# Hybrid encoder trunk on one core: activation operands start 16 to 240 bytes past multiples of 256, and the activation sums are issued over five steps per pair

## The chip, the cores and the metric

One NeuronCore of one Trainium2 chip runs the whole program. The metric is the device time of one execution in microseconds; the median of the kernel before is 2223.44 us (three runs, 2222.92 to 2223.47).

## The reference, cut to what matters

The input is 256 tokens of width 2048 in float32. Layer 0 is a mixer of a bidirectional mLSTM and an RG-LRU, layer 1 is dilated attention, and each is followed by a SwiGLU feed-forward block of width 5632. Nearly all the work is products of activations with weights that are read once from HBM.

```python
for l in range(DEPTH):                       # DEPTH = 2
    h = rmsnorm(x, e_norm[e])                # l = 0
    x = x + even_mixer(h, e_w_in[e], ..., e_w_out[e])
    ...
    h = rmsnorm(x, o_norm[o])                # l = 1
    x = x + dilated_attention(h, o_w_qkv[o], o_w_o[o])
    ...
    h = rmsnorm(x, f_norm[l])
    x = x + swiglu(h, f_w1[l], f_w3[l], f_w2[l])
return rmsnorm(x, final_norm)

def swiglu(h, w1, w3, w2):
    return (jax.nn.silu(h @ w1) * (h @ w3)) @ w2
```

## The kernel before

**Numbers.** Each float32 operand is split into two float32r parts, a high part (ScalarE copies, which rounds) and a low part (VectorE subtracts the high part). A product is then three matmuls on TensorE: high by high, high by low, low by high. Activations are split once when they are made; weights are split as they arrive from HBM, 1 MB (four blocks of 128 rows by 512 columns) at a time.

**Steps.** The program is a list of 768 steps, each half of such a weight block. `emit_step(s)` first issues the splits of the weights for steps up to s + 3 (`AHEAD = 3`, four buffers each for the high and the low parts, so that the split for step s + 4 needs the buffer that step s reads), then the matmuls of step s, then calls `run_tasks` once. There are three kinds of step:
- narrow (536 steps of 12 matmuls): a 128x128 block of activations is the stationary operand, 512 columns of weights move;
- wide (112 steps of 16 matmuls): weights are stationary, and the activations move, 512 and then 256 columns;
- seven (120 steps of 21 matmuls): in the first product of each feed-forward block (all columns but the first chunk's, blocks 4 to 15 of the width), a 2x2 block product is done with seven products of 256 columns in place of eight. It needs sums of weights (`weight_sums`, made together with the split of that block) and sums of activations (`act_sums`).

**Tasks.** Everything that isn't a weight split or a main matmul is a Python generator. `run_tasks` moves each generator on to its next `yield`: first those in `urgent` (evacuations of finished chunks), then up to three of `queue`. What a generator issues between two yields thus stands behind the matmuls of one step and ahead of the splits that the next step issues. Each engine works through its own instructions in the order issued. `until(flag)` calls `run_tasks` again and again until a flag is set, at the moment when the matmuls that need it are issued.

**The sums of activations.** `act_sums` is put in the queue at the first step of each feed-forward block (step 112 for the first). For each of six pairs of width blocks (4, 6, 8, 10, 12, 14) it adds the high and low parts (L1067, VectorE), forms four sums (L1070 to L1073, VectorE), and splits them (L1074 ScalarE, L1075 VectorE): one pair per `run_tasks`. The first chunk of the feed-forward block has 16 narrow steps (112 to 127). The second begins with four more narrow ones; its seven steps are 132, 133, 136, 137, 140 and 141, and they need the pairs in order, pair 1 at step 132 and pair 6 at step 141. In the last step of a chunk (141), the order of the seven products is another: the first one is `sa(0)`, which reads a sum.

**Addresses.** In SBUF, all the tiles that hold activations as operands of these matmuls (`xT`, and the slots of `hT`, `ya`, `yb`, `oT` and `sf`) begin at multiples of 256 bytes, and so do the weight tiles. A slot is 2112 floats (8448 bytes) and the tiles named take 2048 of them. The mLSTM's values `v` stand in a slot with heads 258 floats apart, so all but the first head of a row block begin off a multiple of 256.

Of the kernel before, what the change touches and what calls it, by code (L numbers as in the profile page):

```python
# [9 lines left out]
F32 = mybir.dt.float32  # L10
# [6 lines left out]
S = 256  # L17
P = 128
# [22 lines left out]
SPLIT_BUFS = 4  # L41
AHEAD = 3

SLOTS = 8
SLOT = 2112
EV_BUFS = 10
# [22 lines left out]
def trunk_kernel(ctx: ExitStack, tc: tile.TileContext, a, out):  # L69
# [14 lines left out]
    mxp = ctx.enter_context(tc.tile_pool(name="mxp", bufs=2, space=PSUM))  # L84
    ctx.enter_context(tc.manual_schedule())

    def slot(shape, dt=F32, name="s8"):
        t = s8p.tile([P, SLOT], dt, tag="s8", name=name)
        n = int(np.prod(shape))
        v = t[:, :n]  # L90
        if len(shape) == 1:
            return v
        pat = {2: "p (a b) -> p a b", 3: "p (a b c) -> p a b c", 4: "p (a b c d) -> p a b c d"}[len(shape)]
        return v.rearrange(pat, **dict(zip("abcd"[1:], shape[1:])))
# [44 lines left out]
    ehr = const.tile([MH, MH, P], F32R, name="ehr")  # L139
    ident, upper, lower = cst[:, 0, :], cst[:, 1, :], cst[:, 2, :]  # L140
    ones = const.tile([P, P], F32, name="ones")
    xT = const.tile([P, KB, 2, S], F32R, name="xT")
    hgh = const.tile([P, 16], F32, name="hgh")[:, :RB]

    def transpose(o, i, n=P):
# [408 lines left out]
    def gr_block(b):  # L554
        def gen(ch):
            if b % 4 == 0:
                rg["g"] = m4((4, S), "gr")
            t = rg["g"]
            g = t[:, b % 4, :]
            join(ch.acc[0], g)  # L560
            ch.acc = None
            V.tensor_tensor(g, g, cur["rB"], op=ALU.mult)
            yield
            if b % 4 < 3:
                return
            yield
            A.activation(t, t, AF.Gelu_apprx_tanh)
            yield
            b0 = b - 3
            while not {f"rgh{b0 // 2}", f"rgh{b0 // 2 + 1}"} <= flags:  # L570
                yield
            yt = ys["y", 8 + b0] = slot((4, 2, S), F32R, name="yb")
            V.tensor_tensor(t, t, rg["h"][:, b0:b0 + 4, :], op=ALU.mult)
            yield
            A.copy(yt[:, :, 0, :], t)
            yield
            V.tensor_tensor(yt[:, :, 1, :], t, yt[:, :, 0, :].bitcast(F32), op=ALU.subtract)
            for k in range(4):
                flags.add(f"y{8 + b0 + k}")
            yield  # L580

        return gen
# [233 lines left out]
    def ml_out(c):  # L816
        while not {f"mh{2 * c}", f"mh{2 * c + 1}", f"go{c}"} <= flags:
            yield
        rs = sm(4, "mrs").rearrange("p (a b) -> p a b", a=2)
        V.tensor_scalar(rs, ml["ss"][:, :, 2 * c:2 * c + 2], 1.0 / DV, EPS, op0=ALU.mult, op1=ALU.add)  # L820
        rsf = rs.rearrange("p a b -> p (a b)")
        power(rsf, rsf, 4)
        yield
        yt = slot((4, 2, S), F32R, name="ya")
        ys["y", 4 * c] = yt
        es = []
        for t in range(2):
            y = ev("ya")
            for k in range(2):
                h = 2 * c + k  # L830
                V.scalar_tensor_tensor(
                    y[:, k * DV:(k + 1) * DV], ml["h"][:, t, h, :], rs[:, t, k:k + 1],
                    ml["go"][:, t, h * DV:(h + 1) * DV], op0=ALU.mult, op1=ALU.mult,
                )
            es.append(y)
        yield
        yield from lag()
        for p in range(2):
            ps = tp("yT")
            for k in range(2):  # L840
                for t in range(2):
                    f0 = (2 * p + k) * P
                    transpose(ps[:, k, t * P:(t + 1) * P], es[t][:, f0:f0 + P])
            for k in range(2):
                kb = 2 * p + k
                g = hgh[:, 4 * c + kb:4 * c + kb + 1]
                A.mul(yt[:, kb, 0, :], ps[:, k, :], g)
                V.scalar_tensor_tensor(
                    yt[:, kb, 1, :], ps[:, k, :], g, yt[:, kb, 0, :].bitcast(F32), op0=ALU.mult, op1=ALU.subtract
                )  # L850
                flags.add(f"y{4 * c + 2 * p + k}")
            yield
# [80 lines left out]
    def att_head(h):  # L933
        qk, v, ab = at.pop(("qk", h)), at["v", h // 4], at.pop(("bias", h))
        if h % 4 == 0:
            at["o", h // 4] = slot((4, 2, S), F32R, name="oT")
        yield
        yield from lag()
        yield from take()
        ps = mx("asc")  # L940
        for t in range(2):
            tk = slice(t * P, (t + 1) * P)
            mm3(ps[:, t * S:(t + 1) * S], (qk[:, 0, tk], qk[:, 1, tk]), (qk[:, 2, :], qk[:, 3, :]), True, True)
        yield
        sn = ev("asn")
        st = sm(6, "ast")
        for t in range(2):
            V.tensor_tensor_reduce(
                sn[:, t * S:(t + 1) * S], ps[:, t * S:(t + 1) * S], ab[:, P - t * P:P - t * P + S],
                1.0, 3e38, op0=ALU.add, op1=ALU.min, accum_out=st[:, t:t + 1],  # L950
            )
            A.activation(
                sn[:, t * S:(t + 1) * S], sn[:, t * S:(t + 1) * S], AF.Exp, scale=-1.0, bias=st[:, t:t + 1],
                accum_out=st[:, 2 + t:3 + t],
            )
        give()
        V.reciprocal(st[:, 4:6], st[:, 2:4])
        for t in range(2):
            V.tensor_scalar(
                sn[:, t * S:(t + 1) * S], sn[:, t * S:(t + 1) * S], st[:, 4 + t:5 + t], None, op0=ALU.mult  # L960
            )
        yield
        yield from lag()
        pt = tp("apT")
        for k in range(2):
            for t in range(2):
                transpose(pt[:, k, t * P:(t + 1) * P], sn[:, t * S + k * P:t * S + (k + 1) * P])
        pv = m4((2, CW), "apv", F32R)
        split2(pv, pt.rearrange("p a b -> p (a b)"))
        yield  # L970
        yield from lag()
        yield from take()
        po = mx("apo")
        hs = slice(h % 4 * DH, h % 4 * DH + DH)
        for k in range(2):
            ks = slice(k * S, (k + 1) * S)
            mm3(po[:, :S], (v[:, 0, k, hs], v[:, 1, k, hs]), (pv[:, 0, ks], pv[:, 1, ks]), k == 0, k == 1)
        yield
        split2(at["o", h // 4][:, h % 4], po[:, :S])
        give()  # L980
        flags.add(f"ao{h}")
        yield
# [6 lines left out]
    def ffn(l, gains, nxt):  # L989
# [29 lines left out]
        def up3(c):  # L1019


            def gen(ch):
                while f"up{l}_{c}" not in flags:
                    yield
                es = st.pop(("e", c))
                for t in range(2):
                    V.scalar_tensor_tensor(
                        es[t], ch.acc[t], cur["rstd"][:, t:t + 1], es[t], op0=ALU.mult, op1=ALU.mult
                    )
                ch.acc = None  # L1030
                yield
                yield from lag()
                h = st["h", c] = slot((4, 2, S), F32R, name="hT")
                for p in range(2):
                    ps = tp("hTp")
                    for k in range(2):
                        f0 = (2 * p + k) * P
                        for t in range(2):
                            transpose(ps[:, k, t * P:(t + 1) * P], es[t][:, f0:f0 + P])
                    A.copy(h[:, 2 * p:2 * p + 2, 0, :], ps)  # L1040
                    V.tensor_tensor(
                        h[:, 2 * p:2 * p + 2, 1, :], ps, h[:, 2 * p:2 * p + 2, 0, :].bitcast(F32), op=ALU.subtract
                    )
                    for k in range(2):
                        flags.add(f"h{l}_{4 * c + 2 * p + k}")
                    yield

            return gen
# [7 lines left out]
        def act_sums():  # L1056

            for g in SEVEN:
                while f"xT{gains}_{g}" not in flags:
                    yield  # L1060
                two = slot((2, 4, 2, P), F32R, "sf")
                for j, kb in enumerate((4 * g, 4 * g + 2)):
                    f = two[:, j]
                    v = ev("sa")
# [2 lines left out]
                    V.tensor_tensor(vv, x[:, :, 0, :], x[:, :, 1, :], op=ALU.add)  # L1067
                    a11, a21, a12, a22 = (vv[:, j, t * P:(t + 1) * P] for j in range(2) for t in range(2))
                    w = ev("sb").rearrange("p (k t) -> p k t", k=4)
                    V.tensor_tensor(w[:, 0], a21, a22, op=ALU.add)  # L1070
                    V.tensor_tensor(w[:, 2], a11, a21, op=ALU.subtract)
                    V.tensor_tensor(w[:, 1], w[:, 0], a11, op=ALU.subtract)
                    V.tensor_tensor(w[:, 3], a12, w[:, 1], op=ALU.subtract)  # L1073
                    A.copy(f[:, :, 0, :], w)  # L1074
                    V.tensor_tensor(f[:, :, 1, :], w, f[:, :, 0, :].bitcast(F32), op=ALU.subtract)  # L1075
                    sf[kb] = f
                    flags.add(f"sf{l}_{kb}")
# [260 lines left out]
```

## Time and profile before

| what | value |
|---|---|
| median of three runs | 2223.44 us |
| the profiled execution | 2224.16 us |
| its span in the trace | 2222.4 us |
| TensorE busy | 99% of the span |
| VectorE busy | 72% |
| ScalarE busy | 52% |
| chain that ended last | TensorE 91%, VectorE 4%, ScalarE 3% |
| HBM traffic | 187 GB/s over the span |

The profiled execution lies 0.7 us above the median and 1.8 us above its own span. In this profile a matmul's duration runs from its start to its modelled end, and the next one starts before that end. A busy TensorE therefore tells little; the distance from one start to the next is the time that a matmul costs.

### The profile page before, as it was taken

Reading aid. Unit: us, or ns where it says so; the run is one execution under the profiler, and the core shown is the slowest. Engines: PE = TensorE matmul, PEld = TensorE weight load, DVE = VectorE, ACT = ScalarE, POOL = GpSimd, SP = SyncE. Lnnn points to the kernel's source line nnn. Section 1 sums busy time; section 2 is a strip of 40 time slices with the busy share of each in tenths; the row PEclk is TensorE's granted clock in tenths of the full one; section 3 lists DMA queues with packets and bytes.
Section 4 is the critical chain, followed back from the end, with each engine's and each line's share of the span. In section 5 each row is a group of like instructions: output and inputs, shape, how many; then the busy total and the mean of one; then the engine's idle time right before and its main releaser. Section 6 shows DMA issues by size and latency. Waiting matters only on the chain.

```text
span 2222.4 us, 28893 instructions
## 1 busy us (share of the span) xinstructions
PE 2195.4 (99%) x11492; PEld 1875.3 (84%) x11492; DVE 1592.0 (72%) x2160; ACT 1156.2 (52%) x1555; POOL 22.6 (1%) x37
## 2 busy tenths in 40 slices
PE   9999999999999999999999999998999999999998
PEld 7887887788888888888888888887888888888886
DVE  6877756785787688578666676567867885886686
ACT  5667554554455455445554555444544554554454
POOL 0000000000000000000000000000000000000000
PEclk9999999999999999999999999999999999999999
DMA  7444554555555555555554555454555555555653
GB/s 277 172 146 140 195 201 166 190 200 194 193 190 195 184 196 204 192 204 190 173 193 175 182 185 175 170 171 172 201 195 189 200 197 191 177 205 195 219 192 130
DMA packets 61470, 417.52 MB, mean 188 GB/s; under 512 B 7060, under 2 KB 7956, under 8 KB 12568
## 3 DMA queue, kind: packets, MB, share of 16 engines
q1 hardware_dynamic: 58616, 406.69, 52.7%
q0 software_dynamic: 2288, 8.39, 1.1%
q8 instruction: 90, 1.47, 0.3%
q10 hardware_dynamic: 432, 0.61, 0.1%
q14 instruction: 44, 0.36, 0.0%
HBM read 413.56 MB, written 2.10 MB: 187 GB/s over the span
## 4 chain that ended last, share of the span: by engine, by line
PE 91%; DVE 4%; ACT 3%; issue 1%; DMA 0%; SPq 0%; POOL 0%; POOLq 0%; DVEq 0%; ACTq 0%
PE acc L301 20%; PE acc L302 20%; PE acc L300 20%; PE acc L361 9%; PE acc L362 5%; PE ext L337 3%; PE ext L338 3%; PE ext L336 3%; PE acc L337 2%; PE acc L336 2%; PE acc L338 2%; DVE wl L229 2%; ACT wh L228 2%; PE hTp L146 1%; PE rgp L524 1%
## 5 line engine op out<-in xcount | busy, mean ns | idle before, releaser
L229 DVE TENSOR_TENSOR wl<-raw,wh 128x1024 fp32r<-128x1024 f32 (+1 forms) x770 | 927.7, 1220 | 512.1 <-ACT wh L228 508.1
L228 ACT CAST wh<-raw 128x1024 fp32r<-128x1024 f32 (+1 forms) x770 | 793.9, 1046 | 500.5 <-PE acc L302 364.8
L300 PE MATMUL acc<-wh,xT 128*128 128x512 f32 x1184 | 468.0, 395 | 4.9 <-ACT wh L228 4.8
L301 PE MATMUL acc<-wl,xT 128*128 128x512 f32 x1184 | 463.5, 391 | 9.1 <-DVE wl L229 9.1
L302 PE MATMUL acc<-wh,xT 128*128 128x512 f32 x1184 | 461.3, 390 | 0.0
L361 PE MATMUL acc<-xT,wh 128*128 128x512 f32 x896 | 322.3, 402 | 0.5 <-ACT v L731 0.5
L300 PE MATMUL acc<-wh,hT 128*128 128x512 f32 x704 | 276.1, 392 | 0.0
L302 PE MATMUL acc<-wh,hT 128*128 128x512 f32 x704 | 274.3, 390 | 0.0
L301 PE MATMUL acc<-wl,hT 128*128 128x512 f32 x704 | 274.1, 389 | 0.1
L301 PEld LDWEIGHTS acc<-wl,xT 128*128 128x128 f32 x1184 | 222.6, 188 | 56.0 <-DVE wl L229 13.9
L300 PEld LDWEIGHTS acc<-wh,xT 128*128 128x128 f32 x1184 | 222.6, 188 | 55.1 <-ACT wh L228 10.4
L302 PEld LDWEIGHTS acc<-wh,xT 128*128 128x128 f32 x1184 | 222.3, 188 | 46.7
L362 PE MATMUL acc<-xT,wl 128*128 128x256 f32 x896 | 251.4, 281 | 0.0
L209 ACT CAST wf<-ws 128x512 fp32r<-128x512 f32 x180 | 111.9, 622 | 197.6 <-DVE ws L202 149.0
L361 PEld LDWEIGHTS acc<-xT,wh 128*128 128x128 f32 x896 | 168.4, 188 | 39.8 <-ACT v L731 0.6
L362 PEld LDWEIGHTS acc<-xT,wl 128*128 128x128 f32 x896 | 169.3, 189 | 0.9 <-DVE wl L229 0.3
L302 PEld LDWEIGHTS acc<-wh,hT 128*128 128x128 f32 x704 | 132.1, 188 | 27.7
L301 PEld LDWEIGHTS acc<-wl,hT 128*128 128x128 f32 x704 | 132.3, 188 | 27.5 <-DVE wl L229 0.5
L300 PEld LDWEIGHTS acc<-wh,hT 128*128 128x128 f32 x704 | 132.2, 188 | 26.8
L210 DVE TENSOR_TENSOR wf<-ws,wf 128x512 fp32r<-128x512 f32 x180 | 113.3, 684 | 0.0
L338 PE MATMUL ext<-wf,sf 128*128 128x256 f32 x240 | 67.9, 283 | 0.0
L337 PE MATMUL ext<-wf,sf 128*128 128x256 f32 x240 | 67.9, 283 | 0.0
(278 smaller groups left out, 2721.6 us busy)
## 6 DMA issues: line engine op xcount, KB each, us to landing
raw<-in_w SPq DMA_DIRECT2D x264, 1024.0 KB, 4.9
raw<-in_w_aqk SPq DMA_DIRECT2D x32, 1024.0 KB, 4.9
raw<-in_w_out SPq DMA_DIRECT2D x16, 1024.0 KB, 5.0
raw<-in_w_av SPq DMA_DIRECT2D x16, 1024.0 KB, 4.8
raw<-in_w_o SPq DMA_DIRECT2D x16, 1024.0 KB, 4.9
raw<-in_w_xr SPq DMA_DIRECT2D x8, 1024.0 KB, 7.5
raw<-in_w_qk SPq DMA_DIRECT2D x8, 1024.0 KB, 4.9
raw<-in_w_og SPq DMA_DIRECT2D x8, 1024.0 KB, 4.8
```

Of the source, the lines that this page charges most:

```text
L209: A.copy(f[:, 0], t)
L210: V.tensor_tensor(f[:, 1], t, f[:, 0].bitcast(F32), op=ALU.subtract)
L228: A.copy(hi[:, k], raw[:, k])
L229: V.tensor_tensor(lo[:, k], raw[:, k], hi[:, k].bitcast(F32), op=ALU.subtract)
L300: PE.matmul(acc, xh, hi[:, j, :], start=f, stop=False)
L301: PE.matmul(acc, xh, lo[:, j, :], start=False, stop=False)
L302: PE.matmul(acc, xl, hi[:, j, :], start=False, stop=e)
L336: PE.matmul(o, xh, wh, start=new, stop=False)
L337: PE.matmul(o, xh, wl, start=False, stop=False)
L338: PE.matmul(o, xl, wh, start=False, stop=end)
L361: PE.matmul(acc, wh[:, j, :], x2.rearrange("p a b -> p (a b)"), start=f, stop=False)
L362: PE.matmul(acc[:, :S], wl[:, j, :], x2[:, 0, :], start=False, stop=e)
```

## The change

The tiles of activations get an offset of their own inside their space: 56 floats (224 bytes) for `xT` and for the sums `sf`, 8 floats (32 bytes) for `hT`, 4 floats (16 bytes) for `ya` and `yb`, and 60 floats (240 bytes) for `oT`. `xT` gets 64 floats more room for it. In `act_sums` four yields are added, so that a pair is issued over five calls of `run_tasks`: the first sum; two of the four; the other two; the rounding copy; the low part and the flag. No instruction is added or removed.

```diff
+OFF_X, OFF_H, OFF_Y, OFF_O = 56, 8, 4, 60
-    def slot(shape, dt=F32, name="s8"):
+    def slot(shape, dt=F32, name="s8", off=0):
-        v = t[:, :n]
+        v = t[:, off:off + n]
-    xT = const.tile([P, KB, 2, S], F32R, name="xT")
+    xT = const.tile([P, KB * 2 * S + 64], F32R, name="xT")
+    xT = xT[:, OFF_X:OFF_X + KB * 2 * S].rearrange("p (k i s) -> p k i s", k=KB, i=2)
-            yt = ys["y", 8 + b0] = slot((4, 2, S), F32R, name="yb")
+            yt = ys["y", 8 + b0] = slot((4, 2, S), F32R, name="yb", off=OFF_Y)
-        yt = slot((4, 2, S), F32R, name="ya")
+        yt = slot((4, 2, S), F32R, name="ya", off=OFF_Y)
-            at["o", h // 4] = slot((4, 2, S), F32R, name="oT")
+            at["o", h // 4] = slot((4, 2, S), F32R, name="oT", off=OFF_O)
-                h = st["h", c] = slot((4, 2, S), F32R, name="hT")
+                h = st["h", c] = slot((4, 2, S), F32R, name="hT", off=OFF_H)
-                two = slot((2, 4, 2, P), F32R, "sf")
+                two = slot((2, 4, 2, P), F32R, "sf", off=OFF_X)
                     w = ev("sb").rearrange("p (k t) -> p k t", k=4)
+                    yield
                     V.tensor_tensor(w[:, 0], a21, a22, op=ALU.add)
                     V.tensor_tensor(w[:, 2], a11, a21, op=ALU.subtract)
+                    yield
                     V.tensor_tensor(w[:, 1], w[:, 0], a11, op=ALU.subtract)
                     V.tensor_tensor(w[:, 3], a12, w[:, 1], op=ALU.subtract)
+                    yield
                     A.copy(f[:, :, 0, :], w)
+                    yield
                     V.tensor_tensor(f[:, :, 1, :], w, f[:, :, 0, :].bitcast(F32), op=ALU.subtract)
                     sf[kb] = f
                     flags.add(f"sf{l}_{kb}")
                     yield
```

## Rows read from the trace of the kernel before

**Rows 1.** The page: TensorE's busy time, and its granted clock in 40 slices.
```profile
PE 2195.4 (99%) x11492; PEld 1875.3 (84%) x11492; DVE 1592.0 (72%) x2160; ACT 1156.2 (52%) x1555; POOL 22.6 (1%) x37
...
PEclk9999999999999999999999999999999999999999
```
**Rows 2.** TensorE's groups by shape: count | busy us, mean ns | idle before, releaser.
```profile
L300 PE MATMUL acc<-wh,xT 128*128 128x512 f32 x1184 | 468.0, 395 | 4.9 <-ACT wh L228 4.8
L301 PE MATMUL acc<-wl,xT 128*128 128x512 f32 x1184 | 463.5, 391 | 9.1 <-DVE wl L229 9.1
...
L361 PE MATMUL acc<-xT,wh 128*128 128x512 f32 x896 | 322.3, 402 | 0.5 <-ACT v L731 0.5
```
**Rows 3.** Timeline of TensorE, narrow steps (start, duration, instruction); 44 matmuls left out.
```profile
999.62 0.39 PE L302 MATMUL acc<-wh,xT 128*128 128x512 f32 x1
...
1009.82 0.39 PE L302 MATMUL acc<-wh,xT 128*128 128x512 f32 x1
```
**Rows 4.** Timeline of TensorE, wide steps; between the rows two and two left out.
```profile
95.02 0.40 PE L361 MATMUL acc<-xT,wh 128*128 128x512 f32 x1
...
95.62 0.28 PE L362 MATMUL acc<-xT,wl 128*128 128x256 f32 x1
95.73 0.40 PE L361 MATMUL acc<-xT,wh 128*128 128x512 f32 x1
...
96.08 0.40 PE L361 MATMUL acc<-xT,wh 128*128 128x512 f32 x1
```
**Rows 5.** Timeline of TensorE, a seven step; 20 matmuls left out.
```profile
800.74 0.28 PE L336 MATMUL ext<-wf,sf 128*128 128x256 f32 x1
...
803.26 0.40 PE L300 MATMUL acc<-wh,xT 128*128 128x512 f32 x1
```
**Rows 6.** The view of line 796, the mLSTM's product: min/median/max ns, first and last start.
```profile
L796 PE MATMUL num<-v,w x48: 377/379/484, 136.6 to 262.2; 128*128 128x257 f32 x48
```
**Rows 7.** VectorE's groups by shape: count | busy us, mean ns | idle before.
```profile
L491 DVE SCALAR_TENSOR_TENSOR xc<-xr,cpk,xc 128x256 f32<-128x256 f32 x24 | 11.4, 483 | 0.6
...
L167 DVE SCALAR_TENSOR_TENSOR xT<-xin,cpk,xT 128x256 fp32r<-128x256 f32 x16 | 7.2, 481 | 3.6 <-ACT xT L166 3.6
```
**Rows 8.** Timeline of VectorE: the fourth pair of sums in the first feed-forward block.
```profile
385.68 0.68 DVE L1067 TENSOR_TENSOR sa<-xT 128x512 f32<-128x512 f32 x1
386.40 0.29 DVE L1070 TENSOR_TENSOR sb<-sa 128x128 f32<-128x128 f32 x1
...
387.13 0.29 DVE L1073 TENSOR_TENSOR sb<-sa,sb 128x128 f32<-128x128 f32 x1
388.11 0.69 DVE L1075 TENSOR_TENSOR sf<-sb,sf 128x512 fp32r<-128x512 f32 x1 [0.69 <-ACT sf L1074]
389.06 1.22 DVE L229 TENSOR_TENSOR wl<-raw,wh 128x1024 fp32r<-128x1024 f32 x1 [0.26 <-ACT wh L228]
```
**Rows 9.** Timeline of TensorE across the same pair.
```profile
388.21 0.39 PE L302 MATMUL acc<-wh,xT 128*128 128x512 f32 x1
389.07 0.49 PE L300 MATMUL acc<-wh,xT 128*128 128x512 f32 x1 [0.47 <-ACT wh L228]
390.33 0.50 PE L301 MATMUL acc<-wl,xT 128*128 128x512 f32 x1 [0.77 <-DVE wl L229]
390.67 0.39 PE L302 MATMUL acc<-wh,xT 128*128 128x512 f32 x1
```
**Rows 10.** Timeline of VectorE, second chunk: split, sums of weights, splits of steps 131 to 133.
```profile
419.61 1.23 DVE L229 TENSOR_TENSOR wl<-raw,wh 128x1024 fp32r<-128x1024 f32 x1 [0.70 <-ACT wh L228]
...
422.07 0.68 DVE L202 TENSOR_TENSOR ws<-raw 128x512 f32<-128x512 f32 x1
...
426.53 2.35 DVE L229 TENSOR_TENSOR wl<-raw,wh 128x1024 fp32r<-128x1024 f32 x2
```
**Rows 11.** Timeline of TensorE: the first matmul of step 141.
```profile
453.63 0.28 PE L336 MATMUL ext<-wf,sf 128*128 128x256 f32 x1
```
**Rows 12.** Timeline of ScalarE: the rounding copy of the weights of step 144.
```profile
453.47 1.05 ACT L228 CAST wh<-raw 128x1024 fp32r<-128x1024 f32 x1 [1.05 <-PE acc L338]
```

## The prediction

> **What bounds the kernel now.** I read the page first: TensorE is busy for 99% of the span at the full granted clock in all 40 slices [rows 1]. Its groups by shape show who makes it wait: only splits of weights, 4.8 us for the high and 9.1 us for the low parts [rows 2]. Those idle times understate what a wait costs, because a matmul's modelled end hangs over the gap behind it. So I went to the timeline and took distances between starts. In a narrow step 45 starts take 10.20 us, 226.7 ns each [rows 3]. At 2.4 GHz, the higher of the two clock levels, 512 columns stream in 213.3 ns, so each handover to the next matmul costs 13.4 ns. In a seven step, 21 starts take 2.52 us, 120.0 ns each for 256 columns (106.7 ns), 13.3 ns again [rows 5]. In wide steps three pairs of 512 and 256 columns take 1.06 us [rows 4]; 0.96 us of that is streaming, so six handovers cost 100 ns, 16.7 ns each, and they are uneven: from 95.62 to 95.73, for 256 columns, it is about 5 ns as far as the rounding tells.
>
> So nearly all of the span is a steady beat, and only two things can move it: the beat (part 1 of the change), or the places where it is broken (part 2). The largest breaks beyond the start of the program are in the first chunk of each feed-forward block. One of them [rows 9]: the starts lie 0.86, 1.26 and 0.34 us apart where 0.227 is due, so 0.63 + 1.03 + 0.11 = 1.78 us are lost. The first block has five such breaks (at 380.0, 384.6, 389.1, 393.6 and 398.1 us; the first is 0.2 us shorter), the second has five more from 1501.5 us on. Together 2 x 8.7 = 17.4 us.
>
> **Why the beat breaks there.** A pair of sums stands on VectorE between two weight splits. It starts at 385.68; the next split of weights begins at 389.06, 3.4 us later [rows 8]. ScalarE's copy of the pair waits for the four sums, and behind that copy stands the next copy of weights, so both halves of a weight split are held up. With its split of 1.2 us, a step then needs 4.5 us of VectorE where its matmuls last 12 x 0.227 = 2.72 us.
>
> **Part 2, the sums over five steps.** What it removes: within the first chunk no step gets more than 0.72 us of VectorE besides its split (1.9 of 2.72 us), and ScalarE's copy finds its input made a step earlier. All breaks of the first chunk should go: -8.7 us per block.
>
> What it moves: six pairs now take 30 calls of `run_tasks`, steps 112 to 141. Pair 1 is ready after step 116, pair 5 after step 136, each before the step that reads it (132 and 140). Pair 6 would get its fifth piece after the matmuls of step 141, which are those that read it. So `until` issues that piece at step 141 itself, behind everything that VectorE has been given by then, the split for step 144 included, and TensorE waits for it, since that step's first product is the one with `sa(0)`.
>
> How long that wait is, I worked out as a list of VectorE's work from the split of step 131 (starts at 419.61) to the last piece of pair 6. The split and the evacuation behind it take 422.07 - 419.61 = 2.46 us; a set of weight sums takes 426.53 - 422.07 = 4.46 us, three of them 13.4; the 13 further splits (steps 132 to 144) take 2.35 / 2 = 1.18 us each, 15.3 in all [rows 10]; two low parts of `hT` are of the shape of the pair's last instruction, 2 x 0.69 = 1.4; of the sums, a pair is 0.72 + 1.02 + 0.69 = 2.43 us (first sum, four small ones, low part [rows 8]), so pairs 5 and 6 and the rest of pair 4 are 2 x 2.43 + 1.71 = 6.6. The sum is 39.1 us, and VectorE ends at 458.7 without an idle moment. Step 141 would have started at 453.63 [rows 11]: it is 5.1 us late. Before, the second chunk's VectorE had just enough slack not to be seen, and it is this slack that the moved pieces use up; earlier steps of that chunk take up some of the lateness if a split is late for them, but the sum at step 141 stays. From below, the wait is bounded by the split of step 144: its copy can't start before step 140 frees the buffer, 453.47 [rows 12], and 1.05 + 1.22 + 0.69 us later is 456.4, 2.8 us late. From above, a few waits for ScalarE within the list (0.26 to 0.7 us each where they are seen [rows 8, 10]) may add 1.5 us: 6.6. I take 5.1, which is the sum itself, since the list leaves no room for the lower one.
>
> Net per block: -8.7 + 5.1 = -3.6 us, between -5.9 and -2.1. Twice: -7.2 us (-11.8 to -4.2).
>
> **Part 1, the offsets.** It adds no instruction. All operands of the narrow, wide and seven matmuls begin at multiples of 256 bytes before, so the trace has no row of the changed case. The nearest on TensorE is the mLSTM's product: by the 258 floats between heads, its moving operand begins 0, 8, 16 and so on up to 56 bytes off a multiple of 256, each equally often, and from the shortest to the median of the 48 there are 2 ns [rows 6]. But it is plain float32, and its two passes take their time differently. For VectorE, the convolution reads 256 elements from 0, 4 and 12 bytes off in 483 ns, where an aligned instruction of its shape takes 481 [rows 7]: splits and sums don't slow down. So my value for this part is nothing, by these two rows. Its bounds lie in the handover, the one piece of the beat that isn't streaming. It occurs 536 x 12 + 120 x 21 + 112 x 16 = 10,744 times with an activation operand. The wide rows show that it isn't fixed: it goes from about 5 ns up to a mean of 16.7 [rows 4]. At 5 ns everywhere, the beat loses 8.4 ns x 10,744 = 90 us; at 16.7 in narrow and seven steps too, it gains 3.3 ns x 8,952 = 30 us.
>
> The Trainium skill's page "SBUF — State Buffer" (Who interferes with whom) says that TensorE never waits on another engine at SBUF, and its Specifications count lines of 16 bytes; all four offsets are whole lines, so by that page part 1 is worth nothing. No run here shows it.
>
> **Sum.** Against the profiled execution: 2224.16 - 7.2 = 2217.0. It lies 0.7 us above the median, so I forecast 2216.
>
> **The rivals.**
> A, shorter handover: stationary and moving operands that both begin at multiples of 256 get in each other's way when they are read, and part of the 13.4 ns is one read waiting for the other. For it: the uneven handovers of the wide steps, which repeat in a fixed pattern. Against it: the 13.4 ns are the same for 256 and 512 columns and for all tiles, as a fixed cost would be. At the full 8.4 ns it gives 2126; at a quarter of that, 2194.
> The page "TensorE: Matmul & The Clock Gate" (Back-to-back issue gap) gives a handover of about 2.5 ns at the full clock; the rows here show 13.4 for float32r with a new stationary operand each time. By the page's figure the estimate would be 10.9 ns x 10,744 = 117 us less, 2099.
> B, longer handover: an operand that begins inside a 256-byte block needs one read more, and the handover goes to the 16.7 ns of the wide steps: 2216 + 30 = 2246. From 0.7 ns per matmul on (7.2 us / 10,744) it eats the gain of part 2, and this is the case on the slower side. For it: the beat of [rows 3] and [rows 5] is a whole number of 13.3 ns units (17 and 9), so that a small delay may cost a step of its own. Against it: narrow steps load their stationary operand in the shadow of a 227 ns matmul.
> C, the wait only moves: VectorE's backlog at step 141 is as long as the breaks that went. Then the list must come to 3.6 us more per block than I summed; the time is 2223.
>
> **How the numbers follow.** A few tenths of a per cent can be told apart from no change here; I take 0.2%, 4.4 us. Forecast 0.45 (0.40 faster, 0.05 within, since its low end is -4.2 us); A 0.25, faster; B 0.20 (0.18 slower, 0.02 within); C 0.10 (0.07 within, 0.03 slower). Together faster 0.65, same 0.14, slower 0.21. Faster holds most, so one range: from 2150, which takes in A up to about three quarters of its price, to 2246, the price of B. The forecast's own range is 2211 to 2219.
>
> **What would show it.** Right: the distance of starts in narrow steps stays 226.7 ns and in seven steps 120; the breaks at 380 to 398 us are gone; one break of about 5 us stands ahead of the seventh-product step 141, with TensorE waiting for VectorE's low part of the sums (`sf`). Wrong: another beat anywhere (A if shorter, B if longer), a beat that differs between the tiles with 16, 32, 224 and 240 bytes, or breaks at steps 132 to 140.

## The result: slower by 21 us, because the narrow beat grew by 6.6 ns

The changed kernel takes 2244.35 us (median of four, 2244.0 to 2245.3), the kernel before 2223.37 (median of four): 1.0095 times the time before, 95% interval 1.0083 to 1.0107. The spans in the traces differ by 2242.2 - 2222.4 = 19.8 us.

The page after, with the lines that answer to [rows 1] and [rows 2] (TensorE's high by high, high by low and low by high matmuls of narrow steps are now lines 303 to 305). TensorE waits less than before, 0.9 and 1.3 us where 4.9 and 9.1 stood, and its matmuls have become longer:
```profile
PE 2219.4 (99%) x11492; PEld 1872.0 (83%) x11492; DVE 1589.4 (71%) x2160; ACT 1155.7 (52%) x1555; POOL 22.6 (1%) x37
...
PEclk9999999999999999999999999999999999999999
...
L303 PE MATMUL acc<-wh,xT 128*128 128x512 f32 x1184 | 472.5, 399 | 0.9 <-ACT wh L231 0.7
L304 PE MATMUL acc<-wl,xT 128*128 128x512 f32 x1184 | 468.0, 395 | 1.3 <-DVE wl L232 1.2
...
L364 PE MATMUL acc<-xT,wh 128*128 128x512 f32 x896 | 322.2, 401 | 0.4 <-ACT v L734 0.4
```
What counts is again the distance of starts. The timeline of TensorE after, a stretch of narrow steps with `hT` (32 bytes): 238 distances from the first row to the last, 55.53 us, 233.3 ns each, where [rows 3] have 226.7.
```profile
915.00 0.40 PE L304 MATMUL acc<-wl,hT 128*128 128x512 f32 x1
...
970.53 0.39 PE L305 MATMUL acc<-wh,hT 128*128 128x512 f32 x1
```
A stretch with `oT` (240 bytes) after: 95 distances, 21.70 us, 228.4 ns each.
```profile
1429.45 0.40 PE L303 MATMUL acc<-wh,oT 128*128 128x512 f32 x1
...
1451.15 0.39 PE L305 MATMUL acc<-wh,oT 128*128 128x512 f32 x1
```
And in the seven steps after (224 bytes), 32 distances in 3.73 us, 116.6 ns each: shorter than the 120.0 of [rows 5].
```profile
805.75 0.28 PE L339 MATMUL ext<-wf,sf 128*128 128x256 f32 x1
...
809.48 0.28 PE L341 MATMUL acc<-wh,xT 128*128 128x256 f32 x1
```

The whole ledger, from the starts of all 11,492 matmuls in each trace. A distance over 260 ns in narrow, 150 in seven and 290 in wide steps is taken as a break: the ordinary distance (226.7, 120, 177) goes to the step, the rest to the breaks.

| us | before | after | difference |
|---|---|---|---|
| narrow steps (6,431 distances) | 1463.0 | 1496.9 | +33.9 |
| seven steps (2,520) | 301.8 | 294.2 | -7.6 |
| wide steps (1,792) | 314.0 | 314.0 | 0.0 |
| breaks | 38.5 | 32.1 | -6.4 |
| other matmuls | 94.9 | 94.7 | -0.2 |
| sum of the differences | | | +19.7 |

The ten breaks of the first chunks ([rows 8, 9], 17.4 us) are gone. In their place stands one break at step 141 of each feed-forward block. Who makes TensorE wait, from the view of its waits after (us in total, times, longest):
```profile
PE ext L341 <- DVE sf L1082: 4.6, 2, 2.3
PE ext L339 <- ACT sf L1080: 3.5, 2, 1.8
PE acc L304 <- DVE wl L232: 1.2, 3, 0.8
```
Its place, in the timeline of TensorE after: the first product of step 141 waits for the rounding copy of pair 6, its third matmul for the low part. The distances are 2.06, 0.22, 2.59 us where 0.12 is due, 4.5 us lost.
```profile
448.95 0.28 PE L341 MATMUL acc<-wf,xT 128*128 128x256 f32 x1
451.01 0.39 PE L339 MATMUL ext<-wf,sf 128*128 128x256 f32 x1 [1.77 <-ACT sf L1080]
451.23 0.28 PE L340 MATMUL ext<-wf,sf 128*128 128x256 f32 x1
453.82 0.39 PE L341 MATMUL ext<-wf,sf 128*128 128x256 f32 x1 [2.31 <-DVE sf L1082]
```
The break has a tail. The stretches of the same place (columns: stretch, its length, busy time of PE, PEld, DVE, ACT and POOL with instructions, then the granted clock, DMA share, GB/s): after 5 us with hardly any matmul the granted clock is 0.50, the lower of its two levels (1.2 GHz), for about 3 us. Fourteen matmuls there start 213 ns apart, not 117: another 1.3 us.
```profile
447.00:449.00 2.00, 2.00 (x20) 2.00 (x18) 2.00 (x5) 1.01 (x2) 0.00 (x0) 1.00 0.00 0
449.00:454.00 5.00, 0.92 (x6) 0.51 (x5) 4.23 (x6) 1.57 (x2) 0.00 (x0) 1.00 0.92 295
...
455.00:457.00 2.00, 2.00 (x11) 2.00 (x11) 0.00 (x0) 0.00 (x0) 0.00 (x0) 0.50 0.23 94
457.00:458.00 1.00, 1.00 (x6) 0.91 (x5) 0.00 (x0) 0.84 (x1) 0.00 (x0) 0.55 0.00 0
```

### The profile page after: what moved, and what is told of

Its sections match the earlier page's. It is cut to its first block, busy times and chain, and to the rows that moved or that the text cites. A ratio compares the mean times of both kernels' runs of the same rounds, so it can differ in the third digit from the quotient of the medians.

```text
span 2242.2 us, 28894 instructions
## 1 busy us (share of the span) xinstructions
PE 2219.4 (99%) x11492; PEld 1872.0 (83%) x11492; DVE 1589.4 (71%) x2160; ACT 1155.7 (52%) x1555; POOL 22.6 (1%) x37
## 4 chain that ended last, share of the span: by engine, by line
PE 92%; DVE 5%; ACT 2%; issue 1%; DMA 0%; POOL 0%; SPq 0%; POOLq 0%; DVEq 0%; ACTq 0%
PE acc L303 21%; PE acc L304 21%; PE acc L305 21%; PE acc L364 9%; PE acc L365 4%; PE ext L341 2%; PE ext L340 2%; PE ext L339 2%; DVE wl L232 2%; PE acc L340 2%; PE acc L339 2%; PE acc L341 2%; ACT wh L231 1%; PE hTp L149 1%; PE rgp L527 1%
## 5 line engine op out<-in xcount | busy, mean ns | idle before, releaser
L303 PE MATMUL acc<-wh,xT 128*128 128x512 f32 x1184 | 472.5, 399 | 0.9 <-ACT wh L231 0.7
L305 PE MATMUL acc<-wh,xT 128*128 128x512 f32 x1184 | 467.5, 395 | 0.0
L303 PE MATMUL acc<-wh,hT 128*128 128x512 f32 x704 | 280.3, 398 | 0.0
L305 PE MATMUL acc<-wh,hT 128*128 128x512 f32 x704 | 278.5, 396 | 0.0
```

The lines of the kernel that those rows point to most:

```text
L303: PE.matmul(acc, xh, hi[:, j, :], start=f, stop=False)
L305: PE.matmul(acc, xl, hi[:, j, :], start=False, stop=e)
```

## The experiments

Theory 1 after this result: the offsets alone lengthen the narrow beat, and the five steps alone would have gained. Its first rival: the later writes of the sums disturb TensorE. Two kernels take the change apart.

**The five steps alone** (2219.81 us, ten runs; 0.9983 of the time before, interval 0.9974 to 0.9993).
```diff
-OFF_X, OFF_H, OFF_Y, OFF_O = 56, 8, 4, 60
+OFF_X, OFF_H, OFF_Y, OFF_O = 0, 0, 0, 0
```


> All offsets 0, the sums issued over five steps as in the change. Theory 1 (the offsets alone lengthen the narrow beat): the distance of starts is 226.7 ns in narrow and 120 in seven steps, as in the kernel before; the ten breaks in the first chunks (17.4 us) are gone, two breaks of 4.4 us at step 141 with some 1.5 to 2 us of matmuls at 1.2 GHz behind each are there (12 to 13 us), so 2223.4 - 17.4 + 12.5 = 2218.5 us. Rival (the later sums slow narrow steps down, by engines that write while TensorE reads): the narrow beat stays at 233 ns and the time above 2235.


Narrow steps stand at 226.7 ns, seven steps at 120, the ten breaks are gone, and step 141 loses 4.5 us, with 15 matmuls at the lower clock behind it in the first block and 17 in the second (17 x 94 ns = 1.6 us). The steps are worth -3.5 us.

**The offsets alone** (2247.04 us, four runs; 1.0106, interval 1.0090 to 1.0123).
```diff
                     w = ev("sb").rearrange("p (k t) -> p k t", k=4)
-                    yield
                     V.tensor_tensor(w[:, 0], a21, a22, op=ALU.add)
                     V.tensor_tensor(w[:, 2], a11, a21, op=ALU.subtract)
-                    yield
                     V.tensor_tensor(w[:, 1], w[:, 0], a11, op=ALU.subtract)
                     V.tensor_tensor(w[:, 3], a12, w[:, 1], op=ALU.subtract)
-                    yield
                     A.copy(f[:, :, 0, :], w)
-                    yield
```


> The four offsets of the change, the sums issued in one step per pair as in the kernel before. Theory 1: narrow steps with xT, hT, ya and yb at 233.4 ns, with oT (240 bytes) at 227, seven steps at 116.7, wide pairs at 353; the ten breaks of 17.4 us are back and no break at step 141: 2244.4 + 17.4 - 12.5 = 2249 us. Rival (it takes both parts): the beat is 226.7 and the time near 2223.


The beat is that of the changed kernel (means of 233.2 ns with `xT`, 233.3 with `hT`, 228.4 with `oT`, 116.8 in seven steps), and the waits for splits are back, as in [rows 2]. TensorE's waits in this run:
```profile
PE acc L304 <- DVE wl L232: 8.6, 12, 0.8
PE acc L303 <- ACT wh L231: 3.5, 8, 0.4
```
The offsets are worth +23.7 us. With the -3.5 of the steps that makes +20.2, against +21.0 measured for both.

**Is it the start, or the distance between two starts?** In a narrow step activations are loaded while weights move. Shifting the weights too tells the two apart. Here `xT`, `sf`, `ya` and `yb` start at 224 bytes, `hT` and `oT` at 0, and all split weights at 224 (`pad0` moves them there, `pad1` brings what lies behind them back to multiples of 256).
```diff
+OFF_X, OFF_H, OFF_Y, OFF_O = 56, 0, 56, 0
...
+    pad0 = ctx.enter_context(tc.tile_pool(name="pad0", bufs=1))
     whp = ctx.enter_context(tc.tile_pool(name="whp", bufs=SPLIT_BUFS))
     wlp = ctx.enter_context(tc.tile_pool(name="wlp", bufs=SPLIT_BUFS))
+    pad1 = ctx.enter_context(tc.tile_pool(name="pad1", bufs=1))
...
+    V.memset(pad0.tile([P, 56], F32, name="pad0"), 0.0)
+    V.memset(pad1.tile([P, 8], F32, name="pad1"), 0.0)
```


> xT, sf, ya, yb start 224 bytes past a multiple of 256, hT and oT at 0, and now the split weights (high and low parts) start 224 bytes past one too; the sums of weights stay at 0. Theory R (what counts is how far the stationary operand starts from the moving one inside 256 bytes): narrow steps with xT, ya, yb return to 226.7 ns, those with hT and oT (now 32 bytes ahead of the weights) go to 233.4, as hT at 32 did in the change. Theory S (the stationary operand's own start counts): xT, ya, yb stay at 233.4, hT and oT are at 226.7. Theory M (any operand off a multiple of 256): all narrow steps at 233 or more.


One run, 2233.5 us. Its timeline of TensorE, first with `xT` (48 distances in 10.88 us, 226.7 ns; the last row is the matmul behind them), then with `hT` (238 in 55.53 us, 233.3 ns):
```profile
767.73 0.39 PE L305 MATMUL acc<-wh,xT 128*128 128x512 f32 x1
...
778.61 0.28 PE L341 MATMUL ext<-wh,xT 128*128 128x256 f32 x1
...
908.74 0.39 PE L306 MATMUL acc<-wl,hT 128*128 128x512 f32 x1
...
964.27 0.40 PE L307 MATMUL acc<-wh,hT 128*128 128x512 f32 x1
```
The two have changed places. `xT` at 224 bytes is as fast as at 0 once the weights stand at 224 too, and `hT`, back at 0, has become slow. For the narrow beat it is the distance between the starts of the stationary and the moving operand inside 256 bytes that counts, not where either begins.

**Which distances.** Four kernels, one run each, with other offsets and the weights at 0. The edit is the line of the four offsets; the last three have the sums over four steps (below).

> xT and sf start 64 bytes past multiples of 256, hT 128, ya and yb 192, oT 32; sums over five steps. Theory 64 (only starts off a multiple of 64 count, as an operand read in blocks of 64 bytes would have it): xT, hT, ya, yb at 226.7 ns and oT at 233.4; seven steps at 120. Theory 256 (what counts is the distance from the moving operand inside 256 bytes): values other than 226.7 at 64 and 128 too, up to 233 to 235. Both: oT at 32 bytes shows 233.4 as hT did at 32 in the change; if it shows 227 instead, it is the tile or the place in the program and not the offset that counts.

> Sums over four steps; xT and sf start 96 bytes past multiples of 256, hT 160, ya and yb 48, oT 208, weights at 0. Theory R (the distance between stationary and moving start inside 256 bytes sets the beat): each tile has a beat of its own by its distance, between 226.7 (0) and about 234, the seven steps another than 120 (114.8 was seen at 64 bytes, 116.7 at 224). Theory R1 (0 is the best distance for narrow steps): all narrow beats are above 226.7. Rival: some distance gives less than 226.7.

> Sums over four steps; xT and sf at 128 bytes, hT 80, ya and yb 112, oT 176. Theory R: xT in narrow steps shows what hT showed at 128 bytes in the earlier run (a mean of 232.5 ns), whatever the tile; R1: all narrow beats above 226.7. Rival (the tile or the program's place counts): xT at 128 differs from hT at 128 by over 1 ns.

> Sums over four steps; xT and sf at 192 bytes, hT 248, ya and yb 8, oT 232. Theory R: xT in narrow steps near the 229 ns that ya and yb showed at 192 bytes; hT at 248 and ya at 8 lie between 226.7 and the value at 240 and 16 bytes (228 and 232 to 233) if blocks of less than 16 bytes count, and equal 226.7 if an operand is read in lines of 16 bytes (then 8 is as 0, and 248 as 240). Rival: no order by distance.


They took 2239.4, 2239.6, 2232.4 and 2220.0 us. The mean distance of starts in narrow steps, from all consecutive matmuls of one tile in the trace (without those over 260 ns; about 2,000 to 3,400 for `xT` and `hT`, 170 to 370 for the others, which are rougher):

| bytes from the weights' start | ns (tile) | bytes | ns (tile) |
|---|---|---|---|
| 0 | 227.1 (`hT`, before) | 112 | 233.3 (`ya`, `yb`) |
| 8 | 230.7 (`ya`, `yb`) | 128 | 232.5 (`hT`), 232.6 (`xT`) |
| 16 | 232.1, 231.6 (`ya`, `yb`) | 160 | 233.4 (`hT`) |
| 32 | 233.3 (`hT`), 233.2 (`oT`) | 176 | 230.1 (`oT`) |
| 48 | 233.1, 233.3 (`ya`, `yb`) | 192 | 229.1 (`xT`), 229.3, 229.0 (`ya`, `yb`) |
| 64 | 233.2 (`xT`) | 208, 224 | 232.7 (`oT`), 233.2 (`xT`) |
| 80 | 232.0 (`hT`) | 232, 240 | 231.1, 227.9 (`oT`) |
| 96 | 234.1 (`xT`) | 248 | 233.3 (`hT`) |

At equal distance the tiles agree (32, 128, 192). Zero is the best of the distances tried; 240 hardly differs from it (`oT` itself has 227.7 at 0 before, and 228.4 at 240 in the run with the offsets alone), 192 comes next, and between 240 and 0 the value at 248 is as bad as any. So starts in lines of 16 bytes don't explain it, nor do blocks of 64. The seven steps follow another order: 119.8 at 0, 114.8 at 64, 117.9 at 96, 118.8 at 128, 116.3 at 192, 116.7 at 224. For them zero is the worst. Wide steps took 312.3 to 314.5 us in every trace, whatever the offsets.

These means can hide more than one beat at one distance. At 16 bytes after, 48 matmuls in a row with `yb` start 226.7 ns apart and the others with `yb` 233.3; with the offsets alone all of `yb` has 233.3. So the distance doesn't fix the beat by itself. From the changed kernel:
```profile
333.90 0.39 PE L303 MATMUL acc<-wh,yb 128*128 128x512 f32 x1
...
344.55 0.39 PE L305 MATMUL acc<-wh,yb 128*128 128x512 f32 x1
```

**Which load meets which matmul.** Only the low part of `hT` is moved by 32 bytes, the high part and the weights stay at 0 (sums over four steps).
```diff
-                h = st["h", c] = slot((4, 2, S), F32R, name="hT", off=OFF_H)
+                h = slot((2, 1032), F32R, name="hT")[:, :, :1024]
+                h = st["h", c] = h.rearrange("p i (k s) -> p k i s", k=4)
```


> Sums over four steps, all at multiples of 256 bytes but the low part of hT, which starts 32 bytes past one (the high part at 0). In each group of three matmuls (high by high, high by low, low by high) the first two have distance 0, the third 32. Theory P (the load of the next stationary operand meets the operand that moves at that time): the distance from the second start to the third grows from 226.7 towards 233, the two others stay nearer 226.7. Theory Q (a matmul's own two operands): the distance from the third start to the next grows. If the beat is a pattern over several matmuls, all three change by parts: a mean near 229.


One run, 2220.8 us. A steady stretch in its timeline of TensorE; the low part is the stationary operand of line 305, so its load runs while line 304 moves its weights:
```profile
909.81 0.40 PE L303 MATMUL acc<-wh,hT 128*128 128x512 f32 x1
910.05 0.40 PE L304 MATMUL acc<-wl,hT 128*128 128x512 f32 x1
910.28 0.39 PE L305 MATMUL acc<-wh,hT 128*128 128x512 f32 x1
910.51 0.40 PE L303 MATMUL acc<-wh,hT 128*128 128x512 f32 x1
910.75 0.40 PE L304 MATMUL acc<-wl,hT 128*128 128x512 f32 x1
910.99 0.39 PE L305 MATMUL acc<-wh,hT 128*128 128x512 f32 x1
```
Over all such groups the distance from 303 to 304 is 232.5 ns, from 304 to 305 238.8, from 305 to the next 303 228.4. The largest growth is where theory P has it, but the others grow as well, and the three together are 699.7 ns, as much as three times the 233.3 of a group whose operands are all 32 bytes off (680 at distance 0). One operand of three at a bad distance costs as much as three: a beat is a pattern over several matmuls, not a price per matmul. This run leans to P and doesn't settle it.

**The sums over four steps.** The two pairs of small sums go together, so that 24 calls do and the last comes at step 135 (offsets 0). 2207.92 us, 0.9930 of the time before, interval 0.9913 to 0.9946.
```diff
                     V.tensor_tensor(w[:, 2], a11, a21, op=ALU.subtract)
-                    yield
                     V.tensor_tensor(w[:, 1], w[:, 0], a11, op=ALU.subtract)
```


> Offsets 0; the four small sums are issued together, so a pair takes four calls and pair 6 is ready after step 135, ahead of the first step of that group (140). Theory 1 (the wait at step 141 is only the thirtieth call coming too late): no break at step 141 and no matmuls at 1.2 GHz behind it; the ten breaks of the first chunk are gone too, so 2223.4 - 17.4 = 2206 us, or 2207 with small ones. Rival (VectorE has no room for the later pairs in the second chunk): breaks of 1 to 3 us move to steps 136 to 141 and the time is 2208 to 2214.


The breaks at step 141 are gone with their tails. Some of the rival is there too: splits of the second chunk come a little late (1.1 us in four waits, by TensorE's view of waits in this run), so 15.6 of the 17.4 us are gained.
```profile
PE acc L304 <- DVE wl L232: 1.2, 3, 0.8
PE ext L340 <- DVE wl L232: 1.1, 4, 0.4
```

**Taking the good side of both.** Three kernels on the base of the four steps try to keep narrow steps at distance 0 and the seven steps off it. In the first, the sums of activations alone start at 64 bytes; in the second the weights of seven steps and the sums of weights start at 192 (so all activations, at 0, are 64 bytes ahead), in the third all activations and the weights of narrow and wide steps at 64, the weights of seven steps at 0. The second and third have one evacuation buffer fewer (9), and in the second a pad of 192 bytes, whose lines are left out below, moves the sums of weights.
```diff
+                two = slot((2, 4, 2, P), F32R, "sf", off=16)
```


> Sums over four steps, all activations at multiples of 256 bytes but the sums sf, which start 64 bytes past one; weights at 0. In a seven step 12 of 21 matmuls then have the distance of 64 bytes. Theory R: these take 114.8 ns and the other nine 120 if each matmul stands for itself: 2207.9 - 1440 x 5.2 ns = 2200.4 us; if the beat needs a run of equal distances, less of it, 2204 to 2207.


```diff
+        o = 48 if st["seven"] else 0
+        hi, lo = (
+            p.tile([P, 2 * CW + 64], F32R, tag=n, name=n)[:, o:o + 2 * CW].rearrange("p (k c) -> p k c", k=2)
+            for p, n in ((whp, "wh"), (wlp, "wl"))
+        )
```


> Sums over four steps, activations at multiples of 256 bytes; the split weights of the seven steps alone, and all sums of weights, start 192 bytes past a multiple of 256, so that in every matmul of a seven step the stationary operand starts 64 bytes ahead of the moving one, and in narrow and wide steps both start at the same place. One evacuation buffer fewer (9), for room. Theory R (only the distance counts): seven steps at 114.8 ns, as with xT at 64 bytes, narrow steps at 226.7; 2207.9 - 2520 x 5.2 ns = 2195 us. Rival S (the stationary operand's own start): seven steps at 120 and 2208 us. If the buffer is missed: breaks, and over 2208.


```diff
+OFF_X, OFF_H, OFF_Y, OFF_O = 16, 16, 16, 16
...
+        o = 0 if st["seven"] else 16
```


> Sums over four steps. All activation tiles start 64 bytes past multiples of 256; the split weights of narrow and wide steps too (distance 0), those of the seven steps and the sums of weights start at multiples of 256, so that in seven steps the stationary operand is at 64 and the moving one at 0, as in the run with xT at 64 bytes that showed 114.8 ns. One evacuation buffer fewer (9). Theory R with own starts counting besides the distance (64 against 0 differs from 0 against 192, which showed 117.6): seven steps at 114.8, narrow at 226.7, 2207.9 - 2520 x 5.1 ns = 2195 us. Rival (the 117.6 of the earlier run came from its surroundings, so another thing than the two starts counts): seven steps at 117.6 again and 2201 us.

| kernel | us | of before | interval | narrow `xT`, ns | seven, ns |
|---|---|---|---|---|---|
| `sums_64` | 2204.78 | 0.9916 | 0.9902 to 0.9931 | 227.6 | 118.3 |
| `seven_shift` | 2200.82 | 0.9898 | 0.9881 to 0.9914 | 227.3 | 117.6 |
| `seven_64` | 2201.48 | 0.9903 | 0.9886 to 0.9919 | 227.5 | 117.5 |

Narrow steps stay at their best beat at any common start, 0 or 64, which is a second test of the distance. But in the seven steps the same distance of 64 bytes gives 117.5 here and gave 114.8 where the narrow steps beside them stood at 64 bytes too, so the last two kernels miss the 2195 us of their first theory. The third repeats the starts of that run (inside 256 bytes), so it isn't the starts of the seven steps' own operands.

The mean of 114.8 (`offsets_64_128`) is a mix of two steady beats. Its seven steps come in pairs, and a pair keeps one beat: in 83 of 118 steps it is about 113.4 ns, in 35 it is 117.8, at the same starts. In `seven_64` 8 of 120 steps have the shorter beat. Here are two pairs of `offsets_64_128`, each with the narrow matmul before it, the first of its 42 matmuls and the one behind them: 4.95 us (117.8 ns each) and 4.76 us (113.4).
```profile
595.77 0.39 PE L305 MATMUL acc<-wh,xT 128*128 128x512 f32 x1
596.00 0.28 PE L339 MATMUL ext<-wh,xT 128*128 128x256 f32 x1
...
600.95 0.39 PE L303 MATMUL acc<-wh,xT 128*128 128x512 f32 x1
...
639.48 0.40 PE L305 MATMUL acc<-wh,xT 128*128 128x512 f32 x1
639.72 0.28 PE L339 MATMUL ext<-wh,xT 128*128 128x256 f32 x1
...
644.48 0.39 PE L303 MATMUL acc<-wh,xT 128*128 128x512 f32 x1
```
The narrow distances there alternate between 231 and 236 ns, and the last one before the pair goes with its beat: of 46 pairs that follow a narrow matmul, all 9 behind a distance of 231 ns run at 117.8, and 36 of the 37 behind 233 to 236 at the shorter beat. So the beat of a seven step goes with how it is entered. That run has all ten buffers and shows both beats, so a missing buffer isn't needed for the longer one. No run changes the entry alone, so this is a link and not a shown cause, and why nearly all pairs behind the 226 or 227 ns of `seven_64` have the longer beat stays open. `seven_shift` and `seven_64` are the fastest of all; their intervals overlap.

## Why the prediction was wrong

**The step that failed is the value taken for part 1.** I took nothing for the offsets and kept +30 us as the upper end. They cost 23.7 us, and with that the sign of the whole turned. I let two rows decide, and neither bore on the case. [Rows 6] give durations, not distances of starts, for plain float32. Its distances in the trace before are 215 to 217 ns in 30 of 32 cases, which is twice the 107 ns that 257 columns stream at 2.4 GHz and 1 to 3 ns more; nothing of the 13.4 ns handover is in it that an offset could change. [Rows 7] are VectorE's, which was never in question: its busy time is 1592.0 and 1589.4 us. The row that did bear on it stood in the text: the handover of the wide steps isn't fixed [rows 4]. Over all wide steps of that trace it goes from 5 to 13 ns for 256 columns and from 11 to 28 ns for 512. A cost that changes so from one matmul to the next is one that can be moved, and a case that puts new starts under 10,744 of them should have been weighted by that.

**Rival B had the size and the wrong cause.** Its price, 3.3 ns on narrow and seven steps (+30 us), is near the total, but narrow steps grew by 33.9 / 6,431 = 5.3 ns on average (6.6 where the steady beat holds, nearly none with `oT`), seven steps became shorter and wide ones stayed. And an operand that begins inside a 256-byte block doesn't cost a read more: with the weights shifted alike it costs nothing. The remark that the beat is a whole number of 13.3 ns units (17 and 9) doesn't hold after the change: 233.3 is 17.5 such units.

**Rival A had the kind of cause and the wrong sign.** It held that two operands that both begin at multiples of 256 get in each other's way. That the two starts matter together is what the runs show; but for narrow steps equal starts are the best case, and only the seven steps gain by leaving it. The page "TensorE: Matmul & The Clock Gate" of the Trainium skill (Step-by-step: what each phase is for) says that loading the next tile's weights doesn't steal read bandwidth from the running matmul. The runs here hold no count of bandwidth, but they show that the load isn't without effect on the beat: with the moving operand where it was, moving the operand that is loaded changes it from 226.7 to 233.3 ns. That the reads collide is an explanation, not shown; the traces hold starts, not reads.

**Part 2, step by step.** The breaks of the first chunk went as forecast (-17.4 us). Pair 6 is late at step 141 as forecast, by 4.5 us where the list of VectorE's work gave 5.1, though TensorE waited for ScalarE's rounding copy first and only then for the low part that I had named. Missed was the tail: after 5 us with hardly any matmul TensorE ran at 1.2 GHz for about 3 us. Part 2 alone measured -3.5 us where I had -7.2; the tail takes about 2 x 1.5 = 3 us of the difference. (The spans of the two traces differ by 2217.2 - 2222.4 = -5.2 us, near -17.4 + 2 x (4.5 + 1.5) = -5.4.) The 4.5 us of VectorE for one step of the first chunk should have been 3.4 + 1.2 = 4.6; nothing hangs on it.

**Rival C** (the wait only moves) was half right: 2 x (4.5 + 1.5) = 12 of 17.4 us came back at step 141. That it was the thirtieth call and not VectorE's load is shown by the four steps: VectorE has the same work there, and step 141 has neither the break nor the tail.

## What to carry to other kernels

Where TensorE's matmuls start at a steady distance, look at that distance less the streaming time, and ask what it depends on before changing any operand's address: here the difference between the starts of stationary and moving operands, in bytes inside 256, was worth 1% of the time, and a common start for both was best for 512 columns. An offset that helps one shape (256 columns) can cost more in another, so measure the distance of starts by shape and by tile, and look whether a mean holds one beat or two. When work is spread over calls, count the calls up to the last consumer: one step too many cost 12 us here (2219.8 against 2207.9), part of it in matmuls at the lower clock behind a wait of 4.5 us.

## What the runs showed of the hardware that I had not expected

- The start-to-start distance of float32r matmuls with a new stationary operand each time depends on the distance between the two operands' starts: means from about 227 ns (0 bytes) to 234.1 (96 bytes) for 512 columns in narrow steps, from 114.8 (64) to 119.8 (0) for 256 in seven steps. The wide steps, which take turns between the two widths, take 312.3 to 314.5 us at all the distances tried.
- It is a common pattern of several matmuls: one bad distance in a group of three lengthens the group by 20 ns, as three do (699.7 against 680 ns).
- Equal starts at 224 or 64 bytes give the same narrow beat as at 0.
- The same starts allow more than one steady beat: 113.4 and 117.8 ns for 256 columns at 64 bytes in one kernel, 226.7 and 233.3 ns for 512 columns at 16 bytes in another. Which one a seven step has goes with the last distance before it; what sets that in general was not found.
- After 5 us with six matmuls (one break of 4.5 us in two pieces) the granted clock fell to 0.50 and came back some 3 us later.
